# An encoder block on one core: states out of PSUM by ScalarE, residual rows in another stage, two operands of the opening and one load of the FFN at another place

## The chip, the cores and the metric

The kernel runs on 1 core of one Trainium2 chip. The time is that of one execution on the device, in microseconds (us), and a kernel's time is the median of its runs. PE is the matmul engine, DVE the vector engine, ACT the scalar (activation) engine, POOL the GpSimd engine, and SP the engine that issues most of the DMAs. Each of them works through its own queue in order.

## The reference

One encoder layer on x (1 x 1024 x 1024, float32):

```python
h = layer_norm(x, ln_in_g, ln_in_b)
proj = h @ w_in                                  # 1024 x 11776
aq, ak, av, hq, hf_fwd, hf_bwd, hi, hg, ga, gh = split(proj)
att = dilated_attention(aq, ak, av, slopes)      # 3 groups of 8 heads of 64, mixed to 512
rec = hgrn2(hq, hf_fwd, hf_bwd, hi, hg, lb, ng)  # 8 heads of 128, both directions
merged = sigmoid(ga) * (att @ w_att_up) + sigmoid(gh) * (rec @ w_hgrn_up)
h = layer_norm(ALPHA * h + merged @ w_o, ln1_g, ln1_b)
gate, up = split(h @ w_ffn_in)                   # 1024 x 5632
h = layer_norm(ALPHA * h + (silu(gate) * up) @ w_ffn_out, ln2_g, ln2_b)
```

hgrn2 is a gated linear recurrence in chunks. With a chunk's keys k, values v and decays f, a state S (128 x 128 per head) goes on as S' = diag(d) S + u, where u = k^T v of the chunk and d the chunk's whole decay; the output of a chunk reads the state at its start.

## The kernel before

Every large product is done as three matmuls on float32r parts: an operand is split into a high part (ACT's cast, `w_hi` and the like, L212) and a low part (source minus high part, on POOL or DVE, L222), and `mm3` (L270 to L272) adds hi·hi, hi·lo and lo·hi into one PSUM bank. The two largest projections use a Strassen-Winograd scheme of seven products on halves of the operands, so the activations are needed as eight forms: b11, b21, t1, t2, t3, t4, b22, b12 (the last only inside sums).

The stages, in order:

1. *First stage* (`phase1`). `phase0` is its opening: it normalises x, transposes it and writes the forms `b11, b21, t2, t1, t3, b22, t4` in the order in which `stream` needs them (product p of a tile pair needs form `PRODUCTS[p]`). `stream` is a generator; each step makes one product (12 matmuls of 128x512), while sums and splits of the weights for later steps are prepared three to five steps ahead. `run(n)` in `phase0` lets n steps be emitted. Some forms are lent as scratch first: w11 lies in the tiles of b22's high part, z2 in t4's low part. POOL makes w11 = z2 - w11 (L463) for t3 and w21 = w21 - z2 (L481) for t4.
2. Between the steps of `stream`, generators emit the attention and the recurrence (`hgrn_side`, one per head). A `yield n` leaves n steps of the projection in between. The recurrence's part: gates and decays per direction (`hgrn_dir`), keys transposed (`hgrn_keys`), states (`hgrn_states`), scores (`hgrn_scores`), outputs (`hgrn_out`). All use four PSUM banks (`ps_sd`, tag sd) in turn, so the scores reuse the two banks of the second direction's keys and then the two of its states.
3. After the last unit, `late` counts steps at the end of the first stage: every sixth loads and splits a part of the attention's result (`load_split`), every third makes one row block of the residual (`residual`): ALPHA * LN_in(x), with a load on SP, one ACT instruction, two DVE instructions (L499, L500) and a store issued from ACT's queue (L501).
4. *Second stage* (`phase2`). A first up-projection of eight tiles (att @ w_att_up), a second of eight (rec @ w_hgrn_up), each gated by a tile `tg` loaded through a ring of four buffers (tag st); in the second, every other tile splits one chunk of w_o (`wo_chunk`; high part on ACT, low part on POOL for the first four). Then the product with w_o by token blocks t = 0..7, the residual added, LN1, and the forms of the FFN's input (`h1_blocks`): t1, t2, b11, b21 stay, while t3, b22 and t4 are stored to DRAM (`td`, L1464).
5. *FFN.* The first products of the first three weight pairs are emitted before block 7 is done. `ffn_in` loads b22, t3 and t4 back (L1623), splits them, and goes on. `ffn_out` is the down-projection with LN2.

In `hgrn_states`, u of four (then three) chunks lies in one PSUM bank. A running value E goes from chunk to chunk by two DVE instructions: E*dec1 + u from PSUM (L1170), then times dec0 (L1171; the first chunk only L1168). ACT scales E by dec1 into S, the state that the output reads (L1162). dec0 and dec1 are the two halves of a chunk's decay.

The order of instructions on each engine is not that of the text alone: a planner simulates the program and takes by priority what is ready; `high_priority` moves work ahead, and `behind` and `ordered` make it place one instruction after another, on the same engine or across engines, and set no semaphore: they bind the planner's order, not the engines while they run.

Of the kernel before, what the change touches and what calls it, by code (L numbers as in the profile page):

```python
# [19 lines left out]
D = 1024  # L20
# [55 lines left out]
SMT_PAD = 832  # L76
# [3 lines left out]
class Block:  # L80
# [235 lines left out]
    def phase0(self, pool, work):  # L316
# [145 lines left out]
        for k in range(4):  # L462
            nc.gpsimd.tensor_sub(w11[k], z2[k], w11[k])  # L463
        for k in range(4):
            self.behind(hi("t1", k, t1), h[0].ins.name)
            self.behind(lo("t1", k, t1), h[1].ins.name)
# [4 lines left out]
        for k in range(4):  # L471
            hi("t3", k, w11, diff[:, k:k + 1])
            lo("t3", k, w11, diff[:, k:k + 1])
# [6 lines left out]
        for k in range(4):  # L480
            nc.gpsimd.tensor_sub(w21[k], w21[k], z2[k])  # L481
# [608 lines left out]
    def hgrn_dir(self, h, d, st):  # L1090
# [42 lines left out]
        dec = st["dec", d] = self.smt.tile([128, 2, 8], F32, name="dec", tag="dec", bufs=4)  # L1133
        nc.gpsimd.tensor_copy(dec[:, 0, :], A[:, :, 63 if d == 0 else 0])
        nc.gpsimd.tensor_copy(dec[:, 1, :], B[:, :, 0 if d == 0 else 65])

# [11 lines left out]
    def hgrn_states(self, st, d, kT, vT):  # L1148

        nc, dec = self.nc, st["dec", d]  # L1150
        S = self.slot(6 + d, "hS", (8, 128))
        cs = list(range(8)) if d == 0 else list(range(7, -1, -1))
        E = None
        for b in range(2):
            ps = self.ps_sd().rearrange("p (k c) -> p k c", k=4)
            part = cs[4 * b:4 * b + 4]
            for jj, c in enumerate(part):
                if c != cs[-1]:
                    nc.tensor.matmul(ps[:, jj, :], kT[b][:, c % 4, :], vT[:, c, :], start=True, stop=True)
            for jj, c in enumerate(part):  # L1160
                if E is not None:
                    nc.scalar.activation(S[:, c, :], E, AF.Copy, scale=dec[:, 1, c:c + 1])  # L1162
                if c == cs[-1]:
                    continue

                En = self.sm.tile([128, 128], F32, name="hR", tag="hR", bufs=3)
                if E is None:
                    nc.vector.tensor_scalar(En, ps[:, jj, :], dec[:, 0, c:c + 1], None, op0=OP.mult)  # L1168
                else:
                    nc.vector.scalar_tensor_tensor(En, E, dec[:, 1, c:c + 1], ps[:, jj, :], op0=OP.mult, op1=OP.add)  # L1170
                    nc.vector.tensor_scalar(En, En, dec[:, 0, c:c + 1], None, op0=OP.mult)  # L1171
                E = En
        return S
# [86 lines left out]
    def phase1(self):  # L1260
# [19 lines left out]
        for k in work:  # L1280
# [43 lines left out]
    def phase2(self):  # L1324
        nc = self.nc
        gc, bc = self.col["g1"], self.col["b1"]
        with ExitStack() as es:
# [9 lines left out]
            mp = es.enter_context(self.pool("mp", "right"))  # L1337
# [21 lines left out]
            wo = [[mp.tile([128, KT, HALF], F32R, name=f"wo0{n}") for n in ("hi", "lo")]]  # L1359
            for d in range(8):  # L1360
                t = tgate(8 + d)

# [6 lines left out]
                if d % 2:  # L1369
                    self.wo_chunk(wo[0], d // 2)  # L1370
            for z in (self.recp, self.stp, self.attp):
# [11 lines left out]

            def rest(t, y):

                with self.tc.high_priority(offset=2 * self.evac_ahead if t == 7 else 0):
# [3 lines left out]
                    else:  # L1390
# [3 lines left out]
                                   last=t >= 3)  # L1394
# [53 lines left out]
    def h1_blocks(self, pool, t, v, last=False):  # L1448
# [35 lines left out]
        later(0, "b22", b22)  # L1484

# [17 lines left out]
    def wino_project(self, raws, evac, ahead=0):  # L1503
# [22 lines left out]
        def keep(ps, pool=None, tag="wkeep", bufs=3):  # L1526
            with self.tc.high_priority(offset=self.evac_ahead):
                t = (pool or self.ws).tile([128, HALF], F32, name="wkeep", tag=tag, bufs=bufs)
# [35 lines left out]

    def ffn_in(self):

        nc = self.nc
        with ExitStack() as es:
# [3 lines left out]
            self.abpool = self.pool("abp", "right")  # L1572
            self.abp = self.abpool.__enter__()
            self.fp = fp = es.enter_context(self.pool("ffn", "right"))
# [44 lines left out]
            for i, n in enumerate(("b22", "t3", "t4")):  # L1619
                for k in (0, 2):  # L1620
                    tag = "fgh" if k else "fgl"
                    r = fp.tile([128, 2, HALF], F32, name="t_raw", tag=tag, bufs=2)
                    ins = nc.sync.dma_start(r, self.td[i][:, k:k + 2, :])  # L1623
                    if i == 0:
                        b22_load = ins.ins.name
                    hi, lo = self.xb[n]
# [35 lines left out]
        self.h1p.__exit__(None, None, None)  # L1662
# [234 lines left out]
```

## Time and profile before

| | |
|---|---|
| median of 3 runs | 2090.71 us (2088.48 to 2091.47) |
| the profiled execution: its own time, and its span | 2086.05 us, 2084.2 us |
| mean granted clock of PE | 0.991 |
| PE busy | 2022.3 us (97%) |
| DVE, ACT, POOL busy | 1365.6 us (66%), 928.0 us (45%), 1090.3 us (52%) |

A time in a line of the profile counts from the span's start. A line names the engine, the line of the kernel, the operation, out<-in by the program's names, sizes and how often; in square brackets stands the idle time before it and what ended it. "PE sd L1187 <- DVE hR L1170: 7.8, 4, 2.7" in the list of waits says that PE's instruction of L1187, which writes tile sd, stood still for DVE's instruction of L1170 on tile hR: 7.8 us in all, 4 times, the longest 2.7 us. "SPq" and "ACTq" are the issuing of DMAs, with the time that the issue held its queue. In the table by windows stand the window's length, then for PE, its weight loads, DVE, ACT and POOL the busy time and the number of instructions, then the granted clock of PE as a share of full speed, the DMA engines' busy share and GB/s.

### The profile page before, as it was taken

What the parts mean: (1) busy time and instruction counts of PE and PEld (TensorE: products, weight loads), DVE (VectorE), ACT (ScalarE), POOL (GpSimd) and SP (SyncE); (2) the same over time, 40 slices, a digit from 0 to 9 for tenths busy, and PEclk for the clock granted to TensorE, in tenths of its full rate; (3) what the DMA queues carried; (4) which work ended last, traced back from release to release, by engine and by line L of the source; (5) the groups of instructions that cost most, each with busy time, mean ns of one, the idle gap of its engine ahead of it and who ended that gap; (6) DMA issues with size and microseconds to landing.
All of it is one profiled execution on the core that took longest, in us unless ns stands there. A gap on an engine that the chain in (4) does not pass through costs nothing.

```text
span 2084.2 us, 30889 instructions
## 1 busy us (share of the span) xinstructions
PE 2022.3 (97%) x10974; PEld 1672.3 (80%) x10974; DVE 1365.6 (66%) x2125; ACT 928.0 (45%) x1856; POOL 1090.3 (52%) x907
## 2 busy tenths in 40 slices
PE   7899999999999999999999999999999999999998
PEld 5678888888887888888888788888788888887876
DVE  6967645885368844687444823447867776758778
ACT  6544455443554436554365531244433333334542
POOL 6766644676446663665634864244656666630012
PEclk9999999999999999999999999999999999999999
DMA  5433442445333353344535764344544343347423
GB/s 156 136 121 129 146 127 98 138 141 163 119 127 120 123 168 100 117 133 135 164 102 163 252 231 156 96 134 127 167 134 143 127 148 127 128 157 286 162 91 127
DMA packets 274844, 297.95 MB, mean 143 GB/s; under 512 B 14017, under 2 KB 207362, under 8 KB 274690
## 3 DMA queue, kind: packets, MB, share of 16 engines
q1 hardware_dynamic: 268384, 274.78, 40.6%
q10 hardware_dynamic: 6306, 21.20, 2.7%
q8 instruction: 86, 1.41, 0.3%
q14 instruction: 68, 0.56, 0.1%
HBM read 201.29 MB, written 94.63 MB: 142 GB/s over the span
## 4 chain that ended last, share of the span: by engine, by line
PE 57%; DVE 6%; issue 2%; DMA 2%; ACT 1%; POOL 0%; SPq 0%; ACTq 0%; DVEq 0%; POOLq 0%
PE pj L271 12%; PE pj L270 12%; PE pj L272 12%; PE sd L271 6%; PE sd L270 6%; PE sd L272 6%; PE sd L1210 1%; DVE qd L1125 1%; DVE a L500 0%; DVE hR L1171 0%; DVE gwkeep L222 0%; PE sd L1015 0%; PE sd L966 0%; DVE hR L1170 0%; DMA w<-in_w_ffn_out_dram 0%
## 5 line engine op out<-in xcount | busy, mean ns | idle before, releaser
L222 POOL TENSOR_TENSOR w_lo<-wa,w_hi 128x512 fp32r<-128x512 f32 x272 | 371.6, 1375 | 285.4 <-ACT w_hi L212 261.1
L212 ACT CAST w_hi<-wa 128x512 fp32r<-128x512 f32 x272 | 167.4, 618 | 239.4 <-PE pj L271 146.5
L222 POOL TENSOR_TENSOR w_lo<-wsum,w_hi 128x512 fp32r<-128x512 f32 x88 | 127.3, 1456 | 114.0 <-PE sd L272 60.7
L222 POOL TENSOR_TENSOR w_lo<-f_raw,w_hi 128x512 fp32r<-128x512 f32 x66 | 102.6, 1563 | 52.4 <-ACT w_hi L212 51.2
L208 POOL TENSOR_TENSOR mv<-mv,mhalf 128x1 f32<-128x1 f32 x16 | 10.7, 678 | 207.3 <-DVE mv L207 207.2
L212 ACT CAST w_hi<-wsum 128x512 fp32r<-128x512 f32 x88 | 54.6, 621 | 124.2 <-PE sd L271 116.4
L270 PE MATMUL pj<-xt1hi,w_hi 128*128 128x512 f32 x252 | 99.8, 396 | 3.6 <-ACT wkeep L679 2.0
L272 PE MATMUL pj<-xb22hi,w_lo 128*128 128x512 f32 x252 | 98.8, 392 | 1.1 <-POOL w_lo L222 0.8
L270 PE MATMUL pj<-xb22hi,w_hi 128*128 128x512 f32 x252 | 99.3, 394 | 0.0
L272 PE MATMUL pj<-xt1hi,w_lo 128*128 128x512 f32 x252 | 98.6, 391 | 0.4 <-POOL w_lo L222 0.4
L271 PE MATMUL pj<-xb22lo,w_hi 128*128 128x512 f32 x252 | 98.5, 391 | 0.0
L271 PE MATMUL pj<-xt1lo,w_hi 128*128 128x512 f32 x252 | 98.4, 390 | 0.0
L222 POOL TENSOR_TENSOR w_lo<-ws,w_hi 128x512 fp32r<-128x512 f32 x46 | 67.3, 1468 | 48.8 <-ACT w_hi L212 48.6
L212 ACT CAST gwsum<-a_raw 128x512 fp32r<-128x512 f32 (+1 forms) x78 | 47.6, 615 | 100.6 <-PE pj L271 46.0
L653 POOL TENSOR_TENSOR wa<-wa,wa 128x512 f32<-128x512 f32 x46 | 66.4, 1452 | 49.2 <-DVE wa L652 42.4
L679 ACT COPY wkeep<-pj 128x512 f32<-128x512 f32 x136 | 79.0, 581 | 25.7 <-DVE evh L557 12.9
L222 DVE TENSOR_TENSOR gwkeep<-a_raw,gwsum 128x512 fp32r<-128x512 f32 (+1 forms) x78 | 57.7, 740 | 41.0 <-ACT gwsum L212 38.1
L530 DVE TENSOR_TENSOR evh<-wkeep,pj 128x512 f32<-128x512 f32 x66 | 57.4, 878 | 41.4 <-PE pj L272 29.5
L270 PE MATMUL pj<-xt4hi,w_hi 128*128 128x512 f32 x192 | 77.0, 401 | 3.9 <-DVE evh L541 3.1
L270 PE MATMUL pj<-xt2hi,w_hi 128*128 128x512 f32 x192 | 77.6, 408 | 2.2 <-ACT w_hi L212 2.2
L272 PE MATMUL pj<-xt2hi,w_lo 128*128 128x512 f32 x192 | 77.0, 402 | 2.2 <-POOL w_lo L222 2.2
L271 PE MATMUL pj<-xt2lo,w_hi 128*128 128x512 f32 x192 | 77.0, 401 | 0.9 <-DVE xt2lo L391 0.9
(419 smaller groups left out, 6562.7 us busy)
## 6 DMA issues: line engine op xcount, KB each, us to landing
wa<-in_w_in_dram SPq DMA_DIRECT2D x184, 256.0 KB, 3.2
f_raw<-in_w_ffn_in_dram SPq DMA_DIRECT2D x44, 512.0 KB, 4.0
a_raw<-gd SPq DMA_DIRECT2D x30, 512.0 KB, 3.7
gd<-fc SPq DMA_DIRECT2D x44, 256.0 KB, 2.0
gd<-fs SPq DMA_DIRECT2D x33, 256.0 KB, 2.1
tg<-evh SPq DMA_DIRECT2D x32, 256.0 KB, 3.3
tg<-tg SPq DMA_DIRECT2D x16, 512.0 KB, 4.5
y<-ahs SPq DMA_DIRECT2D x16, 512.0 KB, 4.8
```

Of the source, the lines that this page charges most:

```text
L208: nc.gpsimd.tensor_tensor(mv[:, 2:3], mv[:, 2:3], self.mhalf[:, 0:1], OP.pow)
L212: ins = nc.scalar.copy(hi, src) if eng_hi == "act" else nc.vector.tensor_copy(hi, src)
L222: ins = e.tensor_sub(lo, src, hi.bitcast(F32))
L270: nc.tensor.matmul(ps, whi, xhi, start=first, stop=False, **kw)
L271: nc.tensor.matmul(ps, whi, xlo, start=False, stop=False, **kw)
L272: self.product = nc.tensor.matmul(ps, wlo, xhi, start=False, stop=last, **kw).ins.name
L530: self.left(nc.vector.tensor_tensor(o, self.order_src(add, g, kind), s, OP.add))
L653: nc.gpsimd.tensor_sub(a["a21"], a["a22"], a["a11"])
L679: nc.scalar.copy(t, ps)
L1125: nc.vector.reciprocal(qd[:, c, far], A[:, c])
L1210: nc.tensor.matmul(po[:, jj, :], l, r, start=(n == 0), stop=(n == len(terms) - 1))
```

## The change

Six edits:

- `phase0`: the POOL subtraction for t3 is placed by `behind` after the last low part of t1, which DVE makes, and that for t4 after the last low part of t3.
- `hgrn_states`: ACT copies each u out of PSUM, scaled by dec0, into S; DVE makes one instruction a chunk, E*dec2 + S, all in SBUF, with dec2 = dec0*dec1 (a new column, made by POOL; `SMT_PAD` pays for its bytes); ACT scales E by dec1 in place as before. A head has 2 x 6 DVE instructions here and not 2 x 13, and 2 x 14 ACT instructions and not 2 x 7.
- `residual` runs in the second up-projection, one row block a tile, in a new pool `rows` for its two vectors; the row blocks share the ring `st` with the gates `tg`.
- The first four `wo_chunk` make their low part on DVE.
- `h1_blocks` gets `then`: for block 7, after the stores of t3 and b22 and ahead of the sum and store of t4, the pool `mp` is closed, the FFN's pools are opened and the loads of b22 and t3 are issued (`ffn_again`). `ffn_in` takes these loads and issues only t4's.
- The first two groups' second kept value (`u2`) lies in a tile of `abp` and no longer in the FFN's pool.

```diff
-SMT_PAD = 832
+SMT_PAD = 704
...
         for k in range(4):
-            nc.gpsimd.tensor_sub(w11[k], z2[k], w11[k])
+            self.behind(hi("t1", k, t1), h[0].ins.name)
+            last = lo("t1", k, t1)
+            self.behind(last, h[1].ins.name)
         for k in range(4):
-            self.behind(hi("t1", k, t1), h[0].ins.name)
-            self.behind(lo("t1", k, t1), h[1].ins.name)
+            self.behind(nc.gpsimd.tensor_sub(w11[k], z2[k], w11[k]), last.ins.name)
...
         for k in range(4):
             hi("t3", k, w11, diff[:, k:k + 1])
-            lo("t3", k, w11, diff[:, k:k + 1])
+            last = lo("t3", k, w11, diff[:, k:k + 1])
...
         for k in range(4):
-            nc.gpsimd.tensor_sub(w21[k], w21[k], z2[k])
+            self.behind(nc.gpsimd.tensor_sub(w21[k], w21[k], z2[k]), last.ins.name)
...
-        dec = st["dec", d] = self.smt.tile([128, 2, 8], F32, name="dec", tag="dec", bufs=4)
+        dec = st["dec", d] = self.smt.tile([128, 3, 8], F32, name="dec", tag="dec", bufs=4)
...
+        nc.gpsimd.tensor_mul(dec[:, 2, :], dec[:, 0, :], dec[:, 1, :])
...
-            part = cs[4 * b:4 * b + 4]
-            for jj, c in enumerate(part):
-                if c != cs[-1]:
-                    nc.tensor.matmul(ps[:, jj, :], kT[b][:, c % 4, :], vT[:, c, :], start=True, stop=True)
-            for jj, c in enumerate(part):
-                if E is not None:
-                    nc.scalar.activation(S[:, c, :], E, AF.Copy, scale=dec[:, 1, c:c + 1])
-                if c == cs[-1]:
-                    continue
-
-                En = self.sm.tile([128, 128], F32, name="hR", tag="hR", bufs=3)
+            part = [(jj, c, cs[4 * b + jj + 1]) for jj, c in enumerate(cs[4 * b:4 * b + 4]) if c != cs[-1]]
+            for jj, c, _ in part:
+                nc.tensor.matmul(ps[:, jj, :], kT[b][:, c % 4, :], vT[:, c, :], start=True, stop=True)
+            for jj, c, after in part:
+                nc.scalar.activation(S[:, after, :], ps[:, jj, :], AF.Copy, scale=dec[:, 0, c:c + 1])
+            for jj, c, after in part:
                 if E is None:
-                    nc.vector.tensor_scalar(En, ps[:, jj, :], dec[:, 0, c:c + 1], None, op0=OP.mult)
+                    E = S[:, after, :]
                 else:
-                    nc.vector.scalar_tensor_tensor(En, E, dec[:, 1, c:c + 1], ps[:, jj, :], op0=OP.mult, op1=OP.add)
-                    nc.vector.tensor_scalar(En, En, dec[:, 0, c:c + 1], None, op0=OP.mult)
-                E = En
+                    En = self.sm.tile([128, 128], F32, name="hR", tag="hR", bufs=3)
+                    nc.vector.scalar_tensor_tensor(En, E, dec[:, 2, c:c + 1], S[:, after, :], op0=OP.mult, op1=OP.add)
+                    E = En
+                if after != cs[1]:
+                    nc.scalar.activation(S[:, after, :], E, AF.Copy, scale=dec[:, 1, after:after + 1])
+                    if after == cs[2]:
+                        nc.scalar.activation(S[:, cs[1], :], S[:, cs[1], :], AF.Copy, scale=dec[:, 1, cs[1]:cs[1] + 1])
...
-                    rs = self.residual(self.sp, self.evp)
-                elif late % 3 == 2:
-                    next(rs, None)
...
+            rows = self.pool("rows")
+            rs = self.residual(sp, rows.__enter__())
             for d in range(8):
                 t = tgate(8 + d)
+                next(rs)
...
-                    self.wo_chunk(wo[0], d // 2)
+                    self.wo_chunk(wo[0], d // 2, "dve")
...
+            def follow():
+                mpool.__exit__(None, None, None)
+                self.ffn_pools()
+                self.again = {n: self.ffn_again(n) for n in ("b22", "t3")}
...
         later(1, "t3", t3)
         later(0, "b22", b22)
+        if then:
+            then()
...
-            u2 = keep(product(6, 1, False), *((self.fp, "fu", 2) if ahead < 3 else ()))
+            u2 = keep(product(6, 1, False), *((self.abp, "ab", 2) if ahead < 3 else ()))
...
+    def ffn_pools(self):
+        self.abpool, self.fpool = (self.pool(n, "right") for n in ("abp", "ffn"))
+        self.abp, self.fp = (z.__enter__() for z in (self.abpool, self.fpool))
+
+    def ffn_again(self, n):
+
+        out = []
+        for k in (0, 2):
+            r = self.fp.tile([128, 2, HALF], F32, name="t_raw", tag="fgh" if k else "fgl", bufs=2)
+            out.append((k, r, self.nc.sync.dma_start(r, self.td[("b22", "t3", "t4").index(n)][:, k:k + 2, :]).ins.name))
+        return out
...
+            for n in ("b22", "t3", "t4"):
+                hi, lo = self.xb[n]
+                for k, r, _ in self.again[n] if n in self.again else self.ffn_again(n):
                     self.split(hi[:, k:k + 2, :], lo[:, k:k + 2, :], r, eng_lo="dve")
```

More of the change, by code (lines that the diff above doesn't have):

```diff
@@ L1336, in phase2 @@
             self.rh, self.rl = (rp.tile([128, KT, T], F32R, name=n) for n in ("rec_hi", "rec_lo"))
-            mp = es.enter_context(self.pool("mp", "right"))
+            mpool = self.pool("mp", "right")
+            mp = mpool.__enter__()
             m0 = [self.rawp.tile([128, 2, HALF], F32, name=f"mT0{k}", tag="fraw", bufs=4) for k in range(4)]
@@ L1369, in phase2 @@
                 if d % 2:
-                    self.wo_chunk(wo[0], d // 2)
-            for z in (self.recp, self.stp, self.attp):
+                    self.wo_chunk(wo[0], d // 2, "dve")
+            for z in (rows, self.recp, self.stp, self.attp):
                 z.__exit__(None, None, None)
@@ L1393, in rest @@
                     self.h1_blocks(yp, t, lambda q, v=None: self.transposed(yp, y, q, gc, bc, v, on_act=on),
-                                   last=t >= 3)
+                                   last=t >= 3, then=follow if t == 7 else None)
                 nc.scalar.dma_start(self.n1_d[t], y)
@@ L1446, with h1_blocks @@
                 7: ("s3", "t3"), 4: ("a22", "t4")}
-    def h1_blocks(self, pool, t, v, last=False):
+    def h1_blocks(self, pool, t, v, last=False, then=None):
         nc = self.nc
@@ L1527, in keep @@
             with self.tc.high_priority(offset=self.evac_ahead):
-                t = (pool or self.ws).tile([128, HALF], F32, name="wkeep", tag=tag, bufs=bufs)
+                t = (pool or self.ws).tile([128, D if pool else HALF], F32, name="wkeep", tag=tag, bufs=bufs)[:, :HALF]
                 nc.scalar.copy(t, ps)
@@ L1563, in ffn_raws @@
         return out
+    def ffn_pools(self):
[7 more added lines that the diff above has]
+        return out
     def ffn_in(self):
-        nc = self.nc
+        nc, fp = self.nc, self.fp
         with ExitStack() as es:
@@ L1571, in ffn_in @@
                 self.xb[n] = [hb.tile([128, 4, HALF], F32R, name=f"x{n}{z}") for z in ("hi", "lo")]
-            self.abpool = self.pool("abp", "right")
-            self.abp = self.abpool.__enter__()
-            self.fp = fp = es.enter_context(self.pool("ffn", "right"))
             acts = [None] * NF
@@ L1618, in ffn_in @@
             self.first_evac = [evac_of(f) for f in range(3)]
[L1619 to L1626, printed above, removed]
+            b22_load = self.again["b22"][1][2]
+            for n in ("b22", "t3", "t4"):
+                hi, lo = self.xb[n]
+                for k, r, _ in self.again[n] if n in self.again else self.ffn_again(n):
                     self.split(hi[:, k:k + 2, :], lo[:, k:k + 2, :], r, eng_lo="dve")
@@ L1661, in ffn_in @@
             sums(NF - 1)
-        self.h1p.__exit__(None, None, None)
+        for z in (self.fpool, self.h1p):
+            z.__exit__(None, None, None)
     def ffn_out(self):
```

## The prediction

> **What bounds the kernel now.** I read the busy table of the page first, then the list of waits of PE over the whole span, then the granted clock in short windows behind the longest waits, and last the timeline around each wait.
>
> ```profile
> PE 2022.3 (97%) x10974; PEld 1672.3 (80%) x10974; DVE 1365.6 (66%) x2125; ACT 928.0 (45%) x1856; POOL 1090.3 (52%) x907
> ```
>
> PE is the bound, and the change leaves its products alone. So all that it can win is in the 62 us of the 2084.2 us span in which PE stands still, and in products that run at a lower clock. This is who ends the waits (engine and line that waits, what it waits for, us in total, times, longest):
>
> ```profile
> PE sd L1187 <- DVE hR L1170: 7.8, 4, 2.7
> ...
> PE sd L271 <- DVE xt1lo L390: 3.9, 3, 3.4
> PE pj L270 <- DVE evh L541: 3.1, 1, 3.1
> ...
> PE pj L270 <- ACT w_hi L212: 2.2, 2, 1.5
> ...
> PE pj L270 <- ACT wkeep L679: 2.0, 1, 2.0
> ...
> PE sd L270 <- ACT xb22hi L212: 1.7, 1, 1.7
> ...
> PE pj L270 <- ACT evh L542: 1.2, 1, 1.2
> PE pj L271 <- DVE xt2lo L391: 0.9, 2, 0.6
> PE sd L271 <- DVE xt3lo L222: 0.6, 1, 0.6
> PE sd L270 <- DVE wkeep L1592: 0.6, 1, 0.6
> ```
>
> Four groups belong to the four parts of the change: the hR chain of the recurrence (7.8), the opening (xt1lo 3.9, xt2lo 0.9), the end of the first stage (ACT evh 1.2, and POOL w_lo, whose row stands in part C) and the seam to the FFN (xb22hi 1.7, xt3lo 0.6, wkeep 0.6). A wait costs more than itself, as windows behind five of them show (the clock stands after POOL's busy time):
>
> ```profile
> 64.70:68.00 3.30, 3.08 (x8) 1.87 (x7) 3.10 (x9) 1.28 (x3) 0.94 (x5) 0.50 0.84 263
> ...
> 235.40:238.70 3.30, 3.30 (x14) 2.61 (x11) 1.52 (x3) 1.70 (x4) 2.26 (x3) 0.50 0.27 93
> 662.00:668.70 6.70, 6.07 (x43) 5.19 (x44) 6.26 (x9) 2.42 (x6) 3.23 (x4) 0.50 0.37 121
> 979.50:982.80 3.30, 3.30 (x37) 2.99 (x34) 3.30 (x5) 1.11 (x3) 1.91 (x2) 0.50 0.29 107
> 1180.90:1184.20 3.30, 3.30 (x8) 2.59 (x9) 3.12 (x2) 2.61 (x5) 3.30 (x3) 0.50 0.42 153
> 883.00:889.00 6.00, 3.98 (x22) 3.19 (x21) 6.00 (x7) 2.34 (x5) 5.20 (x5) 1.00 0.41 131
> ```
>
> Behind a wait PE runs at clock 0.50 for 3.3 us (once 6.7), so half of that is lost on top: 1.65 us, or 3.35. Behind the 2.0 us wait at 883 (ACT wkeep) the clock stayed at 1.00, so this is not certain for a wait of 2 us.
>
> [...]
>
> **A, the opening.** Removed from 45 to 60 us: POOL's eight subtractions for t3 and t4, which now stand behind the last low part of t1 and of t3.
>
> ```profile
> L463 POOL TENSOR_TENSOR lent_xb22hi<-lent_xt4lo,lent_xb22hi x4: 1290/1738/1757, 46.0 to 57.0; 128x512 f32<-128x512 f32 x4
> L481 POOL TENSOR_TENSOR v<-v,lent_xt4lo x4: 1731/1742/1747, 47.3 to 58.7; 128x512 f32<-128x512 f32 x4
> L390 DVE TENSOR_TENSOR xt1lo<-lent_xt3hi,xt1hi x4: 678/1752/1774, 57.5 to 65.9; 128x512 fp32r<-128x512 f32 x4
> ...
> 54.92 2.18 ACT L331 ACTIVATE xt1hi<-lent_xt3hi 128x512 fp32r<-128x512 f32 x4
> 70.55 0.61 PE L270 MATMUL pj<-xt3hi,w_hi 128*128 128x512 f32 x2
> L222 POOL TENSOR_TENSOR w_lo<-wa,w_hi 128x512 fp32r<-128x512 f32 x6 | 9.4, 1576 | 10.5 <-ACT w_hi L212 10.5
> ```
>
> DVE's t1 subtraction takes 0.68 us at best and 1.75 with POOL at work, and is what PE waits for. With POOL quiet the last t1 low part can be ready at 57.1 + 0.7 = 57.8, and all of 3.9 + 0.9 + 1.65 = 6.45 us would go: PE would reach t3 at 64.1 and not at 70.55. But t3 is now late. From 57.8 POOL needs four subtractions (1.29 to 1.74 each) and two w_lo (1.3 to 1.7): 65.4 to 68.2. So t3 makes PE wait 1.3 to 4.1, and 2.3 to 5.1 are left. Next, t4's four subtractions run between POOL's w_lo, whose idle time of 10.5 us (the last row, over 60 to 83 us) they mostly use up; ACT has t4's casts ahead of the next w_hi, and the loads behind it already make PE wait 2.2 (ACT w_hi). A lead of more than about 2 us is lost there. And `behind` sets no semaphore: it binds the planner, while on the chip POOL starts what its own queue lets it. Only a w_lo in front that waits for its w_hi holds the subtractions back; without one they run as early as now and nothing is won. I take 2.0; bounds -2 (nothing won, a new clock stretch of 1.65) and 6.45.
>
> **B, states out of PSUM by ACT.**
>
> ```profile
> L1162 ACT ACTIVATE hS<-hR,dec x112: 384/402/413, 145.7 to 981.2; 128x128 f32<-128x128 f32 x112
> L1170 DVE SCALAR_TENSOR_TENSOR hR<-hR,dec,sd x96: 328/347/351, 145.7 to 978.9; 128x128 f32<-128x128 f32 x96
> L1171 DVE TENSOR_SCALAR hR<-hR,dec x96: 275/288/1362, 146.1 to 980.1; 128x128 f32<-128x128 f32 x96
> 220.66 1.72 PE L1159 MATMUL sd<-hv,hkT 128*128 128x128 f32 x14
> 229.16 0.32 PE L1184 MATMUL sd<-qd,t 128*64 128x128 f32 x1
> 234.25 0.27 PE L1187 MATMUL sd<-qd,t 128*64 128x64 f32 x1 [2.72 <-DVE hR L1170]
> 242.68 0.38 PE L1210 MATMUL sd<-hv,ham 128*128 128x128 f32 x2
> ...
> 1430.42 1.16 ACT L308 ACTIVATE tsv<-sd,vc 128x128 f32<-128x128 f32 x3 [1.49 <-DVE xt2lo L222]
> ```
>
> A state bank is free when the last hR step that reads it is done: two DVE instructions a step, 0.35 and 0.29 to 1.36 us. PE's scores need the bank at 234.25 - 2.72 = 231.5 and get it at 234.25. Afterwards ACT empties a bank with four or three copies. The recurrence shows no scaled copy out of PSUM by ACT; the nearest row of that size, engine and source is L308 in the later normalisation, three in 1.16, so 0.39 each. I take 0.40, as for hS's scaling out of SBUF, with bounds 0.39 and 0.6 (L308's with its semaphores between). The 14 copies of a head then take 5.5 to 8.4 us from 220.66 + 1.72 = 222.4, when PE has made the states: free at 227.9 to 230.8, with 0.40 at 228.0, before 231.5. That takes out 7.8 us of waits and half of 3.3 + 6.7 + 3.3 = 13.3 us of clock, 6.65: 14.4 in all. The price: 7 more ACT instructions a direction, 112 x 0.40 = 45 us on an ACT that is 45% busy; DVE gives up at least 96 x 0.29 = 28 us. The 16 tiny POOL products hide beside PE. I take 13; bounds 4 (the wait passes to ACT in two of four heads and with it most of the clock) and 14.4.
>
> [...] The old L1170 had one input in PSUM and never took over 0.35; the new one reads both from SBUF. [...]
>
> **C, residual rows and wo.** In the first stage's last 50 us, DVE takes 1.2 to 3.4 us for a row's step, and ACT, whose queue issues the row's store, stands behind it with a w_hi that PE needs. The first row is PE's wait for POOL between 1150 and 1200 us; a w_lo can start only behind its w_hi:
>
> ```profile
> PE pj L272 <- POOL w_lo L222: 3.9, 3, 2.2
> L500 DVE SCALAR_TENSOR_TENSOR a<-binb,a x8: 1210/2192/3408, 1142.2 to 1192.0; 128x1024 f32<-128x1024 f32 x8
> 1178.77 0.62 ACT L212 CAST w_hi<-wa 128x512 fp32r<-128x512 f32 x1 [4.00 <-DVE a L500]
> ...
> 1253.00:1324.00 71.00, 71.00 (x315) 58.80 (x314) 22.32 (x26) 11.97 (x17) 27.46 (x18) 1.00 0.44 134
> 1282.67 0.62 ACT L212 CAST w_hi<-w_raw 128x512 fp32r<-128x512 f32 x1 [7.53 <-PE pj L271]
> w_raw<-in_w_hgrn_up_dram SPq DMA_DIRECT2D x6, 512.0 KB, 4.4
> ```
>
> Gone are 3.9 + 1.2 + 1.65 of clock = 6.75 us. At the new place the rows find DVE busy 22 of 71 us and ACT 12. Eight rows bring DVE 2 x 2.2 each and four wo low parts, of the same size, 2.2 at most: 44 us more, 66 of 71 with all of it at the slow end. ACT's store waits there too, but w_hi is cast 7.5 us after ACT fell idle, when PE frees the tile, a projection ahead of its use. DVE's first row waits for its two vectors' load; behind it stands the evacuation of PE's banks, of which there are four. What hides all this is PE's 71 us of products; without it the price is the last rival. I take 6; bounds 3 (POOL's attention splits, which stay, keep half) and 6.75.
>
> **D, b22 ahead of t4's store.**
>
> ```profile
> 1448.18 0.51 SPq L1464 DMA_DIRECT2D td<-tsv  x1
> 1452.32 6.81 SPq L1464 DMA_DIRECT2D td<-tsum  x2
> 1459.30 1.97 SPq L1623 DMA_DIRECT2D t_raw<-td  x4
> ```
>
> SP holds t4's store until 1459.1, and the four loads behind it; b22 itself was stored at 1448. Issued behind t3's store they start some 6 us earlier. They stand ahead of t4's store, which waits for t3's landing at most; t4 is not ready before. 1.7 us go for sure, and of DVE's 0.6 + 0.6, which is a backlog, half: 2.3; bounds 0.5 and 2.9.
>
> **E, a new order.** The instruction order comes from a planner that simulates time, so it moves all over the first stage. Waits like the evh at 3.1 and the wkeep at 2.0 can come or go, and ACT is fuller. I take -1.5; bounds -5 and +3.
>
> **Sum.** 2.0 + 13 + 6 + 2.3 - 1.5 = 21.8. The profiled execution took 2086.05 us (span 2084.2); it becomes 2064.3. The median of the runs, 2090.71, lies 4.7 above it, and I carry that over: 2068.9. Own range 2062 to 2075.
>
> **The rivals.**
> - The bank's wait changes hands: ACT is in order, and hS scalings that wait for DVE stand ahead of the copies. For: ACT already follows hR step by step. Against: copies need only PE. B gives 4: 2090.7 - 12.8 = 2077.9. Chance 0.13.
> - The new order makes two waits like that of evh, 3.1 + 1.65 each: 9.5 less, 2078.4. For: that wait has no cause but order. Against: DVE loses 28 us of work. Chance 0.13.
> - What is won is lost in the next wait, because loads and POOL set the pace: 3 us are left, 2087.7. For: POOL in the opening. Against: PE is at 97%, and other stages show no wait. Chance 0.05.
> - Slower: tg tiles and rows now share one ring of four buffers in the second up-projection, and SP, in order, holds the next weights behind a tile that is not free. The price if they come only on demand: 4.4 (landing) + 0.6 (cast) + 1.6 (low part) = 6.6 in six of eight projections, 39.6: 2108.5. It decides from 21.8 / 6 = 3.6 us a projection. Against: the 7.5 us above. Chance 0.07.
>
> **How the numbers follow.** The forecast has 0.62. Range 2060 (all upper bounds of A to D: 30.5 us) to 2083: outside are the last two rivals, and some 0.08 of tails. Faster by over 0.2% (4.2 us, about what can be told from no change): 0.62 + 0.13 + 0.13 = 0.88; within: 0.05; slower: 0.07.
>
> **What would show it.** A: xt1lo gone from PE's waits, xt3 or w_lo at 64 to 68 us in its place. B: no wait for hR; if one for hS at L1184 or L1187 stands there, the first rival. C: no w_lo wait before the up-projection, clock 1.00 there, and none for w_raw's w_hi behind it. D: t_raw issued ahead of the last td store. I am wrong if PE's idle time stays near 60 us, or if it falls by 20 and the clock's half stretches stay.

## The result, and the profile after

The changed kernel takes **2071.8 us** (median of 4 runs, 2071.3 to 2074.5) against 2089.6 beside it: a ratio of **0.992, 95% interval 0.9902 to 0.9937**. The forecast was 2068.9, its own range 2062 to 2075. The profiled execution took 2071.3 us with a span of 2069.5; the profiled one of before took 2086.05 with a span of 2084.2, so the two traces differ by 14.7 us, where the medians differ by 17.8.

The busy table of the changed kernel, which answers the one quoted of before:

```profile
PE 2016.2 (97%) x10974; PEld 1669.0 (81%) x10974; DVE 1325.4 (64%) x2017; ACT 953.8 (46%) x1968; POOL 1074.7 (52%) x919
```

DVE gave up 40 us, ACT took on 26. PE stands still for 53 of 2069.5 us, where it was 62: of the 14.7 us, 8.6 are idle time. The other 6.1 are busy time of the same products: the granted clock stood at half for 38.5 us in before's trace and for 26.7 in this one, and half of that difference is 5.9. PE's waits (engine and line that waits, what it waits for, us in total, times, longest):

```profile
...
PE pj L270 <- DVE evh L531: 4.3, 3, 2.4
PE pj L272 <- POOL w_lo L222: 4.0, 3, 2.5
PE sd L271 <- DVE xt1lo L390: 2.7, 2, 2.3
PE sd L270 <- ACT xt1hi L212: 2.6, 1, 2.6
PE pj L271 <- DVE w_lo L222: 2.4, 1, 2.4
PE pj L270 <- ACT wo1hi L212: 2.1, 1, 2.1
...
PE sd L271 <- DVE xb22lo L391: 1.9, 3, 0.7
```

No row names hR, hS, xb22hi or xt3lo any more. In their stead stand wo1hi and xb22lo of L391, which before did not have, xt1hi, which cost 0.5 there, and an evh of L531 with a wait of 2.4, where the longest of that line (L530 there) was 1.4. In the recurrence two small waits grew, for ham (1.1, before 0.2) and for hkT (1.1, before none). The clock (the number behind POOL's) in windows behind four waits of now (61.7, 1335, 1440.8, 2017.7) and at the places of before's stretches:

```profile
61.70:65.10 3.40, 3.06 (x8) 1.96 (x7) 3.20 (x10) 1.43 (x3) 0.88 (x5) 0.50 0.90 266
...
231.00:234.30 3.30, 3.30 (x16) 2.71 (x16) 0.52 (x1) 0.59 (x2) 2.68 (x3) 1.00 0.67 204
650.00:656.70 6.70, 6.70 (x98) 5.98 (x98) 6.18 (x8) 3.60 (x9) 4.28 (x3) 1.00 0.24 85
967.00:970.30 3.30, 3.30 (x66) 3.02 (x62) 3.30 (x5) 2.05 (x6) 1.61 (x2) 1.00 0.23 79
1161.00:1164.30 3.30, 3.30 (x16) 2.71 (x16) 1.87 (x2) 1.32 (x3) 1.78 (x2) 1.00 0.21 79
1335.00:1338.30 3.30, 3.30 (x9) 2.55 (x9) 0.93 (x2) 0.00 (x0) 0.00 (x0) 0.50 0.54 160
1440.80:1444.10 3.30, 3.30 (x9) 2.57 (x8) 3.27 (x3) 0.00 (x0) 2.18 (x2) 0.50 0.81 279
2017.70:2021.00 3.30, 3.30 (x10) 2.56 (x9) 3.30 (x6) 1.14 (x2) 0.00 (x0) 0.50 0.73 251
```

All four stretches of B and C are gone, and so is the one that before has behind its evh wait (clock 0.50 from 119.25 to 122.66 us). Three new ones stand at the start of the wo product (1335), at the seam to the FFN (1441) and behind a wait for w_lo near the end (2017.7), which before has too, at full clock (1.00 from 2027.3 to 2037.5 us).

To see where the time went I compare the moments at which PE has done the same work (columns streamed so far; PE's work is the same in all kernels). Before's profiled execution is a fast one of its kernel (2086.05 us, where the medians of before lie between 2089.0 and 2090.7), so at the end of the span these differences are 2 to 6 us less favourable to the other kernels than the medians are. The left column is before's time in us, the others say how much later (+) or earlier (-) each profiled kernel is there; the four in the middle are the experiments with one part alone:

```
before    A only   B only   C only   D only    after
   20       0.4     -0.5      1.9      0.5      0.0
   70      -2.0      0.1      2.1      1.1     -3.0
  110       1.6      0.1      2.3     -0.1      2.3
  150      -4.2     -4.5      2.2     -0.1     -3.6
  260      -4.1     -8.4      2.6      0.4     -7.7
  680      -5.7    -12.3      2.1     -1.5    -12.2
  700      -5.4     -8.8      2.1      1.8    -10.3
 1150      -4.0    -10.6      1.4      2.4    -12.5
 1190      -3.8    -12.2     -5.9      2.4    -19.9
 1360      -3.6    -11.5     -0.4      2.5    -15.4
 1460      -3.6    -11.5     -0.5      5.8    -11.4
 1490      -2.4    -10.4      0.6      1.1    -15.7
```

Read down the last column: the opening *loses* 2.3 by 110 us, 5.9 are won by 150, the recurrence wins some 9 by 1150, the end of the first stage 7.4; then the wo product gives 4.5 back and the seam first loses 4 and wins 4.3. (C's 2 us stand there at 20 us already, ahead of any of its edits.)

### The profile page after: what moved, and what is told of

The parts are those of the page before. It is cut to its first block, busy times and chain, and to the rows that moved or that the text cites. A ratio compares the mean times of both kernels' runs of the same rounds, so it can differ in the third digit from the quotient of the medians.

```text
span 2069.5 us, 30921 instructions
## 1 busy us (share of the span) xinstructions
PE 2016.2 (97%) x10974; PEld 1669.0 (81%) x10974; DVE 1325.4 (64%) x2017; ACT 953.8 (46%) x1968; POOL 1074.7 (52%) x919
## 5 line engine op out<-in xcount | busy, mean ns | idle before, releaser
L222 POOL TENSOR_TENSOR w_lo<-wa,w_hi 128x512 fp32r<-128x512 f32 x272 | 363.2, 1345 | 277.8 <-ACT w_hi L212 250.3
L542 DVE TENSOR_TENSOR evh<-wkeep,pj 128x512 f32<-128x512 f32 x45 | 30.8, 684 | 106.4 <-PE pj L272 61.2
L531 DVE TENSOR_TENSOR evh<-wkeep,pj 128x512 f32<-128x512 f32 x66 | 57.5, 879 | 44.5 <-PE pj L272 33.9
L270 PE MATMUL pj<-xb11hi,w_hi 128*128 128x512 f32 x192 | 76.8, 402 | 1.3 <-DVE wkeep L556 1.3
```

What stands on the lines that cost most here:

```text
L222: ins = e.tensor_sub(lo, src, hi.bitcast(F32))
L270: nc.tensor.matmul(ps, whi, xhi, start=first, stop=False, **kw)
L531: self.left(nc.vector.tensor_tensor(o, self.order_src(add, g, kind), s, OP.add))
L542: self.left(nc.vector.tensor_add(t, add, ps))
```

## The experiments

**One part alone, on the kernel before.** Each takes only its own hunks of the diff: A those of the opening, B those of the states and `dec`, C those of the residual rows and `wo_chunk`, D the FFN's pools and loads. One line of each is shown:

```diff
 # a_only: the opening alone            # b_only: dec, hgrn_states, SMT_PAD
+            self.behind(nc.gpsimd.tensor_sub(w11[k], z2[k], w11[k]), last.ins.name)
+                nc.scalar.activation(S[:, after, :], ps[:, jj, :], AF.Copy, scale=dec[:, 0, c:c + 1])
 # c_only: rows, wo low parts           # d_only: follow, ffn_pools, ffn_again
+                next(rs)
+                self.again = {n: self.ffn_again(n) for n in ("b22", "t3")}
```

> The kernel before with part A alone (the subtractions for t3 and t4 behind the last low part of t1 and of t3). Theory: A by itself loses. PE reaches its first product with t3 3 to 5 us earlier than the 70.6 us of before, but t4's four subtractions now meet xb22lo on DVE and w_lo on POOL, and at the work that before has done at 110 us this kernel is 2.3 us late; the 3.1 us wait for evh at 114.6 us in the trace of before belongs to A's neighbourhood in the order, so it goes too, and the end is 2 to 4 us earlier: 2086. Rival: that wait goes only with the other parts' order; then A ends 0 to 2.5 us later than before: 2090 to 2092. Second rival, the prediction's: A wins 2.0 for good by its own route, with t3 waiting for its late sums: 2087.6 and PE ahead at 110 us.

> The kernel before with part B alone (states out of PSUM by ACT, the states' products of the decays by POOL). Theory, from the two traces: the waits for hR (7.8 us) and the half clock behind them go, new waits in the same heads give some 3 us back, and B is worth 11 us: 2078.6. The prediction's step: 13 us, 2076.6. Rival: half of what the heads show comes from the new order and not from the states; then 4 to 6 us: 2084 to 2086, with hR gone from the waits all the same.

> The kernel before with part C alone (residual rows in the second up-projection, low parts of the first half of wo on DVE). Theory: it wins 7.4 us at the end of the first stage and gives 4.1 back where the wo product begins (PE waits for wo1hi for 2 us and its clock falls), because rows and wo low parts stand ahead of PE's last evacuations on DVE and hold the loads of wo's second half: -3.3, 2086.3. Rival: the wait for wo1hi comes from the order that the other parts make; then C alone shows none and is worth 6 to 7.4: 2082 to 2083.5.

> The kernel before with part D alone (b22 and t3 loaded ahead of t4's store, the FFN's pools opened there). Theory: the waits for xb22hi, xt3lo and wkeep (2.9 us) go, but with the FFN's pools open earlier the first groups' evacuations come ahead of the last block's chain on DVE, PE waits 2.5 us for xt1hi at 1435 to 1451 us and runs 3.4 us at half clock: 0, within 1.5 us of before (2089.6). Rival, the prediction's step: no such wait, because it comes from the other parts' order; D is worth 2.3 to 2.9: 2087.

Measured, beside a before of 2089.0 (ratio and its 95% interval in brackets): A **2083.5** (0.9973, 0.9963 to 0.9983), B **2075.7** (0.9937, 0.9919 to 0.9955), C **2088.5** (0.9999, 0.999 to 1.0009), D **2085.6** (0.998, 0.997 to 0.999). Against what was expected, A is 2.5 us faster, B 2.9, and D 4.0; C is 2.2 slower.

*A* loses 1.6 by 110 us and then, by 150, is 4.2 ahead, since before's wait of 3.1 us for evh (L541) at 115 us is gone with its half clock. *B* shows that too. Its list of waits has these two rows for evh of that line and the one of L530:

```profile
PE pj L270 <- DVE evh L530: 4.3, 3, 2.4
...
PE pj L270 <- DVE evh L541: 0.6, 1, 0.6
```

So that wait hangs on nothing that A or B is about; either one seems to reshuffle the order enough to lose it. C and D, whose edits come later in the program, keep it. Each of the two single runs counts its 4.5 to 5.8 us; together they can win them only once. The four ratios multiplied give 0.9889, which is 23 us; measured were 17. The wait counted twice is of the size of that gap of 6, but so is the gap's uncertainty from the five intervals, so this is the likely cause and not a shown one.

*C* is worth nothing by the times, and its trace has the theory's two sides: 7.3 us won by 1190, 5.5 lost by 1360. Its DVE and ACT around the end of the second up-projection (start, duration, engine, line; in brackets the idle time before and what ended it):

```profile
1328.48 1.22 DVE L499 SCALAR_TENSOR_TENSOR a<-a,ginb 128x1024 f32<-128x1024 f32 x1 [3.44 <-ACT a L498]
1329.74 1.22 DVE L500 SCALAR_TENSOR_TENSOR a<-binb,a 128x1024 f32<-128x1024 f32 x1
1330.89 0.68 DVE L1365 SCALAR_TENSOR_TENSOR tg<-tg,pj 128x512 f32<-128x512 f32 x1
...
1337.22 1.28 DVE L1366 TENSOR_TENSOR mT<-mT,tg 128x512 f32<-128x512 f32 x1
```

```profile
1327.21 1.24 ACT L498 ACTIVATE a<-a,mv 128x1024 f32<-128x1024 f32 x1 [4.06 <-DMA a<-in_x_dram]
...
1335.73 1.64 ACT L212 CAST w_hi<-mT 128x256 fp32r<-128x256 f32 x5 [3.28 <-DVE mT L1366]
1337.27 2.00 ACT L212 CAST wo1hi<-w_raw 128x1024 fp32r<-128x1024 f32 x2
```

DVE stands idle for 3.4 us in front of the last row's step, because ACT's normalisation waits for the row's load. PE's evacuations (L1365, L1366) queue behind it; the last of them ends at 1338.5. ACT, in order, casts w_hi late and wo1hi behind it, 2.1 us after the wo product began at 1335.1. In before it was 0.6 us. The loads of wo's last two pieces wait for that cast's buffers and go out some 2 us later; PE waits 2.2 us for their wo1hi; in the changed kernel, where that wait is 2.1, a stretch at half clock stands behind it (0.50 from 1334.9 us).

*D* shows the wait for xt1hi by itself. Its DVE, around the last block's chain (L310 and L1477 on the block's side, L1602 and L1604 the FFN's first evacuations):

```profile
1445.88 0.67 DVE L1602 TENSOR_TENSOR fc<-wkeep,sd 128x512 f32<-128x512 f32 x1
1447.26 0.69 DVE L1604 SCALAR_TENSOR_TENSOR fth<-fth,fc 128x512 f32<-128x512 f32 x1 [0.70 <-ACT fth L1603]
...
1450.07 0.68 DVE L1602 TENSOR_TENSOR fc<-wkeep,pj 128x512 f32<-128x512 f32 x1
1450.66 0.72 DVE L310 TENSOR_SCALAR tsv<-sd,vc 128x128 f32<-128x128 f32 x2
1451.71 1.35 DVE L1604 SCALAR_TENSOR_TENSOR fth<-fth,fc 128x512 f32<-128x512 f32 x1 [0.33 <-ACT fth L1603]
...
1453.31 1.47 DVE L1477 TENSOR_TENSOR tsum<-tsv,xb11hi 128x512 f32<-128x512 f32 x1
```

In before all FFN evacuations came behind the block's chain. With the pools opened earlier their tiles are free earlier, and the planner places them between. In place D loses 3.3 and wins 4.7: 1.4 us. By the times it is worth 3 to 4; its profiled execution, at 2088.9 us the longest of the ten, does not show that difference. Between 680 and 700 us, outside D's place, it loses 3.3 against before; its longest wait for evh of L530 is 2.2 us, where before's is 1.4. What D is worth alone stays open.

**Mending one part each, on the changed kernel.** The sums for t3 and t4 go to DVE; the rows get buffers of their own; the first FFN evacuations go behind the last block's low part of t1; and all three.

```diff
 # t3_on_dve (and the same for w21)
-            self.behind(nc.gpsimd.tensor_sub(w11[k], z2[k], w11[k]), last.ins.name)
+            self.behind(nc.vector.tensor_sub(w11[k], z2[k], w11[k]), last.ins.name)
 # rows_own_ring: residual, per half h of a row
-            a = pool.tile([128, D], F32, name="a0", tag="st", bufs=4)
...
+            for h, tag in enumerate(("wsum", "wkeep")):
...
+                a = self.ws.tile([128, HALF], F32, name="a0", tag=tag, bufs=3)
 # evac_behind: evac_of, first three groups; self.tail is the last low part made in put(), that of t1
-                        nc.vector.tensor_add(c[:, s], add, ps)
+                        ins = nc.vector.tensor_add(c[:, s], add, ps)
+                        if f < 3:
+                            self.behind(ins, self.tail)
```

> The changed kernel (2071.8 us), with the eight subtractions for t3 and t4 on DVE, still behind the last low part of t1 and of t3: there DVE's own queue holds them, and POOL is quiet beside DVE. Theory: in the changed kernel POOL runs them ahead of where they were meant and beside DVE's low parts, which so take 1.75 and 5.9 us (the group at xb22lo) where they could take 0.7 and 3.8; with DVE's queue the 2.3 us lost by 110 us come back and the waits for xt1lo (2.3), xb22lo (1.9) and w_lo at 88 to 95 us (3.7) shrink: 3 to 5 us less, 2067 to 2069. Rival: t3 now waits for four more steps on DVE, and the order behind 100 us brings the 3.1 us wait for evh back with its half clock: 2072 to 2075.

> The changed kernel (2071.8 us), with the residual rows in buffers of their own (in halves of 512 columns, three of each), not in the ring of four that they share with the tg tiles. Theory: in part C a row's load waits for a buffer, lands 4 us later, and ACT's normalisation and DVE's first step, placed early in in-order queues, hold PE's evacuations behind them (DVE idle 3.4 us in front of the last row); so mT and w_hi are late at the start of the wo product, and wo1hi is 2.1 us late. With rows loaded ahead this idle time goes, wo1hi is in time, the 2.1 + 0.5 us of waits shrink to about 0.5 and the half clock behind them (1.7) goes: 3.5 to 4 us less, 2068. Rival: the wo low parts on DVE make the backlog; then the wait stays: 2071 to 2072.

> The changed kernel (2071.8 us), with the first three FFN groups' evacuations on DVE placed behind the last block's low part of t1 (part D had let them go ahead). Theory: five FFN steps of 0.7 us each and what ACT does for them stand ahead of the last block's transposed copies on DVE and make xt1hi late; behind them, PE's wait for xt1hi goes from 2.6 to 0.5 us and the half clock after it (1.7 us) goes: 3.8 less, 2068. Rival: the last block's chain is late for another reason (the loads of part D on SP, ACT's share of the copies), or the wait moves to the FFN's wkeep tiles and banks: 2070.5 to 2072.

> The changed kernel with all three edits: subtractions on DVE, rows in buffers of their own, FFN evacuations behind the last block. Theory: the three stages lie apart, so the three gains add: 10 to 12.5 us less than the changed kernel, 2059.5 to 2062. Rival: a gain is lost where the order of later work changes, 2064 to 2068.

Measured beside a before of 2089.8: t3_on_dve **2068.2** (0.9899, 0.9885 to 0.9912), rows_own_ring **2074.1** (0.9932, 0.9918 to 0.9946), evac_behind **2073.3** (0.9924, 0.9906 to 0.9941), all_three **2069.5** (0.9906, 0.9892 to 0.992). Only the first came out as expected. By the times the other three cannot be told from the changed kernel (0.992); they missed their forecasts by 6, 5 and 7.5 us or more, and the combination its rival's 2064 to 2068 too.

*The opening.* In the changed kernel POOL ran the sums like this, with DVE's low part of b22 beside the second group:

```profile
49.11 1.29 POOL L222 TENSOR_TENSOR w_lo<-ws,w_hi 128x512 fp32r<-128x512 f32 x1 [2.85 <-ACT w_hi L212]
50.36 6.40 POOL L467 TENSOR_TENSOR lent_xb22hi<-lent_xt4lo,lent_xb22hi 128x512 f32<-128x512 f32 x4
...
67.71 5.51 POOL L482 TENSOR_TENSOR v<-v,lent_xt4lo 128x512 f32<-128x512 f32 x4
```

```profile
71.92 5.89 DVE L391 SCALAR_TENSOR_TENSOR xb22lo<-lent_xt4hi,vc,xb22hi 128x512 fp32r<-128x512 f32 x4
```

The sums of t3 start right behind a w_lo, 5 us *ahead* of t1's first low part (55.5 us), although they are ordered behind its last. On DVE they take half the time, and xb22lo a fifth less:

```profile
57.98 3.58 DVE L467 TENSOR_TENSOR lent_xb22hi<-lent_xt4lo,lent_xb22hi 128x512 f32<-128x512 f32 x4
66.48 2.49 DVE L482 TENSOR_TENSOR v<-v,lent_xt4lo 128x512 f32<-128x512 f32 x4
...
69.06 4.80 DVE L391 SCALAR_TENSOR_TENSOR xb22lo<-lent_xt4hi,vc,xb22hi 128x512 fp32r<-128x512 f32 x4
```

The first product with t3 moves from 65.2 to 61.5 us, and at the work of 110 us this kernel is some 6 ahead of the changed one; 3.5 are left at the end. Two things change at once here: the order of the sums, and POOL's absence beside DVE. No run separates them.

*Rows in their own buffers* took the wait for wo1hi away: its first cast comes 0.6 us behind the start of the wo product, as in before. But now nothing held the rows, the planner put six half rows in one lump into the first up-projection, and PE waited there for the mT evacuation behind them (between 1190 and 1250 us of the table above this kernel loses 7.6 us):

```profile
PE pj L270 <- DVE mT L1357: 5.5, 2, 4.1
```

*The evacuations behind the block* brought xt1hi down to 0.5, as expected, and a new wait up, as the rival had it, though for another tile than it named:

```profile
PE sd L271 <- DVE xb22lo L222: 2.0, 1, 2.0
```

*All three together* keep the opening's gain (3.2 us ahead of the changed kernel at 1150), and lose 6.7 to the mT wait and 2.0 to the one for xb22lo.

**A second round**, with the changed kernel beside it once more. rows_spread joins t3_on_dve and rows_own_ring and holds each row's first DVE step behind the evacuation before it; spread_without_D takes D back; spread_t4_on_pool has evac_behind, and the last block's two steps for t4 on POOL.

```diff
 # rows_spread; self.evicted is the last mT evacuation written so far
-                nc.vector.scalar_tensor_tensor(a, a, ALPHA, gb[:, s], op0=OP.mult, op1=OP.mult)
+                self.behind(nc.vector.scalar_tensor_tensor(a, a, ALPHA, gb[:, s], op0=OP.mult, op1=OP.mult), self.evicted)
 # spread_t4_on_pool, in h1_blocks
+        e = nc.gpsimd if then else nc.vector
-        nc.vector.tensor_sub(t4, hi, t2)
...
+        e.tensor_sub(t4, hi, t2)
...
```

> The changed kernel once more, as the measure for the three kernels beside it: 2071.8 us, 2070 to 2074. It also tests a reading of the clock taken from the ten traces so far: in each of them the stretches of half clock begin whole multiples of 3.413 us apart and last 3.41 or 6.83 us, and they follow a cell of this grid in which PE stood still for more than about 1.8 us. If that holds, all stretches of this trace lie on one grid too, and the 2.4 us wait for w_lo at 2010 to 2020 us and the 2.6 us wait for xt1hi at 1436 cost a stretch or none by where they lie on it, not by their length. If the clock went by the length of a wait, the same waits as in the first trace would have stretches behind them at the same delay.

> The changed kernel with the subtractions for t3 and t4 on DVE, and with the residual rows in buffers of their own, now with each row's first step on DVE held behind the evacuation before it in the program, so that one row falls to each projection. Theory: the wait for mT in the first up-projection (4.1 + 1.4 us in the run with rows in buffers of their own) came from three rows' steps placed there in one lump; spread out, both that wait and the one for wo1hi (2.1 us) stay away. 3.5 from the opening and 4 from wo1: 2064. Rival: DVE has too little room for rows and wo low parts in the second up-projection, and another wait comes there: 2067 to 2070.

> As rows_spread, with part D taken back (b22, t3 and t4 loaded behind t4's store, the FFN's pools opened only there). Theory: D exchanges the waits for xb22hi, wkeep and xt3lo (3.7 us, with little half clock) for the one for xt1hi (2.6 us) and the half clock after it, and is worth nothing: within 1.5 us of rows_spread. Rival: D is worth the 2.3 us of the prediction or the 4 us that it gave alone, and this kernel is that much slower.

> As rows_spread, with the first FFN groups' evacuations behind the last block's low part of t1, and the last block's two steps for t4 on POOL. Theory: at the seam DVE has work without a pause from 1436 to 1456 us, so an order of its steps only says which tile is late (xt1hi in the changed kernel, xb22lo with the evacuations held back); with 3.5 us of it moved to POOL both are in time: PE waits for xt1hi 0.5 us and for xb22lo under 0.6, no half clock there, some 4 us less than rows_spread: 2060. Rival: POOL's w_lo become late behind the two steps, or xb22lo stays late for its load: equal to rows_spread within 1.5 us.

Measured beside a before of 2089.0: the changed kernel **2072.8** (0.9919, 0.9902 to 0.9937), rows_spread **2065.6** (0.988, 0.986 to 0.990), spread_without_D **2065.1** (0.9886, 0.9869 to 0.9904), spread_t4_on_pool **2063.9** (0.988, 0.9861 to 0.9899).

By their times the first three came out as expected; spread_t4_on_pool missed its 2060 by 4 us, and lies where its rival put it.

*rows_spread* beats both kernels, by 7 us the changed one. Its trace shows that the opening does most of it: at 600 us it is 4.7 us ahead of the changed kernel's first execution and 5.3 ahead of its second. The wait for mT is away, but wo1hi still costs 1.5. What holds DVE now is the other half of C:

```profile
1303.90 1.23 DVE L222 TENSOR_TENSOR wo0lo<-w_raw,wo0hi 128x1024 fp32r<-128x1024 f32 x1 [10.01 <-ACT wo0hi L212]
1305.04 1.78 DVE L1371 TENSOR_TENSOR mT<-mT,tg 128x512 f32<-128x512 f32 x1
```

DVE stands for 10 us in front of a low part of wo whose weights have not landed (ACT's cast before it waits 5.4 us for them), with an evacuation behind it. So the theory behind rows_own_ring, rows alone, seems to be half of it, and its rival, the wo low parts on DVE, to hold as well. That is read from this trace: no run here has spread rows and these low parts back on POOL. The wait differs between kernels with the same code at this place (1.4, 1.5 and 2.3 us in the last three), and between the two executions of the changed kernel (2.1 and 1.7).

*D* is worth nothing in this company that can be told: without it the kernel is within 0.6 us, and the two intervals are 4 us wide to either side. *t4 on POOL* brings xt1hi to 0.5 and leaves xb22hi at 1.1 and xb22lo at 1.7 us: no gain of its own that the intervals can tell. The first half of the theory, that another order only says which tile is late, fits all three orders seen here; that DVE's load alone is to blame does not.

## Why the prediction was right, and where not

The total was near, but partly by luck: four of the five terms were forecast too high, and a new order and a fast trace of before made up for much of it. By its own steps:

- **A, +2.0: wrong, it lost 2.3 in place** (1.6 alone), just outside the lower bound of -2. The reservation that the order binds the planner only, and that POOL starts what its queue lets it, is what happened (49.1 and 50.4 above): the wait for xt1lo fell only from 3.9 to 2.7. By 76 us the changed kernel is 3.0 ahead, and it loses that in two places. The first is a step that failed: t4's subtractions would "mostly use up" POOL's idle time. They did, and beside them DVE's four low parts of b22 took 5.9 us and not 3.8 (three that ran beside a POOL instruction 1.76 to 1.86 each, the fourth, with none beside it, 0.74), and PE waited 1.9 for them (3.9 lost by 80 us). I had priced such steps for t1, at 0.68 and 1.75, and forgot them at the place the work moved to. The second is POOL's order (3.2 lost between 92 and 96 us): a step of the recurrence stands ahead of a w_lo, which in before came first, and PE waits 3.7 us for w_lo between 71 and 113 us, where it was 0.4. A alone has 2.4 there. That would belong to E. (The prediction's earliest time for t3 sums to 65.6, not 65.4.)

```profile
92.91 2.65 POOL L1110 TENSOR_SCALAR t<-t,gna,ga 128x1024 f32<-128x1024 f32 x1
...
95.67 1.26 POOL L222 TENSOR_TENSOR w_lo<-wa,w_hi 128x512 fp32r<-128x512 f32 x1
```

- **B, +13: the mechanism right, the size 2 too high.** Alone 13.3 by the medians, but 4.5 of that is the lost evh wait; its heads gave about 11 both alone and in the changed kernel (5.0 around 235 us, 4.1 around 660, 2.0 around 975). Two of its steps in the changed kernel (instructions that touch hS; ns, least, median, most), and the group of the second (busy us, mean ns):

```profile
L1163 ACT ACTIVATE hS<-sd,dec x112: 348/378/417, 141.9 to 964.5; 128x128 f32<-128x128 f32 x112
...
L1169 DVE SCALAR_TENSOR_TENSOR hR<-hR,dec,hS x80: 340/352/1454, 143.1 to 968.4; 128x128 f32<-128x128 f32 x80
```

```profile
L1169 DVE SCALAR_TENSOR_TENSOR hR<-hR,dec,hS 128x128 f32<-128x128 f32 x80 | 44.4, 555 | 12.9 <-ACT hS L1172 6.8
```

  The copy took 0.38 where I had put 0.40. A mean of 0.555 over a median of 0.352 says that some DVE steps took far longer (21 of 96 over 1 us, the worst 1.45). All 21 ran beside a POOL instruction, while of the 68 that took under 0.5 us only 7 met one. Before's L1171, which reads hR alone beside dec, took over 1 us in 17 of 96 steps, each time beside POOL, the longest 1.36; its L1170, which reads u from PSUM, met POOL in 36 of 96 and took 0.35 at most. Nothing hung on the slow steps: no wait of PE names hR or hS.
- **C, +6: right at its first place, wrong at its second.** The end of the first stage gave 7.4, 0.6 above the upper bound. But "What hides all this is PE's 71 us of products" failed. I had compared busy times (22 of 71 us); what matters in an in-order queue is what its head waits for. A step that hangs on a load stood there and PE's evacuations behind it (in C's own trace DVE stood 3.4 us in front of the last row's step). The price was 4.5 us, so C is worth 2.9 in this kernel; alone, its times show nothing. The slow rival had the right place, the shared ring, but not the mechanism: the up-projection's weights were never late for PE, and it cost 4.5 and not 39.6.
- **D, +2.3: wrong, 0.3.** The old waits went, as costed. The step that failed is that I costed loads only: opening the FFN's pools earlier also lets other work in, and then xt1hi is late (2.6 us and a half-clock stretch, 0.50 from 1440.7 us).
- **E, -1.5: wrong in sign, and outside its upper bound of +3.** The evh wait that I called order without a cause vanished, +5.9 between 110 and 150 us, and another one of 2.4 came at 682 us, -1.9: +4.0. That second wait stands at 2.4 in all ten traces of kernels with B, and at the same work with 2.2 in D alone; before, A and C have none there. So it may as well be a price of B, which would leave B 9 and E 5.9. The runs do not settle it.

Against the sum of 21.8, A, C and D fell 9.4 short and B 2, and E gave 5.5 more: 15.9. Another 1.1 is lost near the end, to the half-clock stretch at 2017.7. To rounding, that makes the 14.7 between the two traces. From trace to trace the forecast was 7 us off: 2064.3, and 2071.3 came. By the medians it is only 2.9 off, because I carried over 4.7 us from before's profiled execution to its median, and the changed kernel's profiled execution lies at its median. That is luck, and so is E's gain. Of the rivals' waits, hS at a bank and weights on demand did not come; of the two new evh waits one did. The prediction's signs for B, C and D came: no wait for hR or hS, clock 1.00 before the up-projection, and t_raw issued at 1438 us, ahead of the last td store at 1444. That for A did not: xt1lo still costs 2.7.

## What to carry to other kernels

A busy share does not say whether an in-order engine has room (DVE was busy 22 of 71 us, and the rows and low parts put there cost 4.5): before work is moved into its queue, ask what each moved step waits for and what stands behind it; a step that hangs on a load belongs behind the evacuations, or on an engine that evacuates nothing. An order given to this planner, which sets no semaphore, held on the chip here only within one engine's queue: POOL began t3's sums at 50.4 us, ahead of DVE's first low part of t1 (55.5), and in t3_on_dve DVE began them at 58.0, behind its last (56.3). And gains that are measured one part at a time need not add where each also shakes the same order: here they make 23 us, and 17 were measured.

## What the runs showed of the clock

What I had not expected: in each of the two traces of the result, the half-clock stretches begin **whole multiples of 3.413 us** apart. In before's they begin at 37.33, 64.64, 119.25, 235.31, 661.97, 979.41, 1180.80 and 2078.50 us: with a cell of 3.4133 us, 8.0, 24.0, 58.0, 183.0, 276.0, 335.0 and 598.0 cells behind the first. In the changed kernel's they begin at 37.84, 61.73, 1334.90, 1440.71, 2017.57 and 2065.35 us: 7.0, 380.0, 411.0, 580.0 and 594.0 cells. Each lasts 3.41 or 6.83 us, one or two cells; the last one of each trace runs into the end.

With cells laid so, whether a stretch follows goes with PE's idle time within the cell before it. Of the 1169 cells at full clock between 30 and 2050 us of these two traces, 11 held 1.90 us or more of idle time, and all 11 were followed by a stretch; six held 1.42 to 1.60, and none was; of the 1152 below, one was (these amounts move by 0.1 us at most where a cell's edge is put 0.1 us elsewhere). That one is the stretch behind xt1hi at the seam of the changed kernel: the wait of 2.6 us lies across two cells, with 1.5 and 1.2 us. It does not fit the 1.8 us that the text on after_again names, and why it comes is open.

So waits of one length stand with a stretch behind them and without. The wait for w_lo near the end is 2.4 us in before and in both executions of the changed kernel. In the changed kernel's trace above, 1.9 of it fell into one cell, and the clock behind it was 0.50 (2017.7), half of 3.41 us lost. In before it lay across two cells, with 1.2 us in each, and the clock behind it was 1.00, as it was in the second execution of the changed kernel (before's window first, then that execution's):

```profile
2034.10:2037.50 3.40, 3.40 (x15) 2.52 (x14) 3.40 (x6) 1.48 (x3) 0.00 (x0) 1.00 0.82 286
```

```profile
2015.00:2018.40 3.40, 3.40 (x14) 2.58 (x15) 3.40 (x5) 1.14 (x2) 0.00 (x0) 1.00 0.41 154
```

The evh wait at 682 us, 2.4 in the changed kernel, had 1.4 in its fullest cell, and the clock behind it was 1.00. The 2.0 us wait at 883 us of before, which the prediction left open, had 1.4 there too and kept the clock.

The mean clock also differs between the runs of one kernel, whose times lie 2 to 12 us apart. The five runs of rows_spread show it best: 2058.5 us at a mean clock of 0.998, 2062.4 at 0.996, 2065.6 at 0.994, 2067.0 and 2067.9 at 0.993. A mean clock lower by 0.005 is 10 us of such a run, about the whole difference.
